# A hybrid encoder step: the attention output stays on the chip, branch B's input is split by column halves, and DeltaNet's key transposes ask for free banks

## The chip, the cores and the metric

One NeuronCore of a Trainium2 chip runs the whole program: TensorE (PE) for matrix products, VectorE (DVE), ScalarE (ACT) and GpSimd (POOL) for elementwise work, SyncE (SP) to issue most transfers. The metric is the device time of one execution in microseconds (us), the median over runs.

## The reference

One layer over 528 prompt rows (16 learned rows and 512) and 64 rows of a second sequence, width 1024, in float32. Two token mixers run in parallel on one projection and are merged under gates; a squared-ReLU MLP follows.

```python
h = rmsnorm(x, norm1)
qa, ka, va, qkv_b, z_b, beta_b, alpha_b, gate_a, gate_b = split(h @ w_in)
# A: differential attention, 8 heads, two 64-wide softmax maps per head, 128-wide values
o_a = rmsnorm((softmax(q1 k1 + bias) - lam * softmax(q2 k2 + bias)) @ va, sub_norm) * (1 - lam_init)
# B: gated DeltaNet, 8 heads of 128, causal conv of width 4, delta rule in blocks
o_b = rmsnorm(gated_delta(silu(conv(qkv_b)), g, beta, state), gdn_norm) * silu(z_b)
mix = sigmoid(gate_a + b0) * (o_a @ w_br_a) + sigmoid(gate_b + b1) * (o_b @ w_br_b)
x = x + mix @ w_out
x = x + square(relu(rmsnorm(x, norm2) @ w_up)) @ w_down
```

Outputs are the new rows of both sequences, the normed keys and the values, the DeltaNet states and the last rows before the convolution.

## The kernel before

Every float32 product of a projection is made of three fast ones: each operand is split into a high part (ScalarE copies it into `float32r`) and a low part (VectorE or GpSimd subtracts), and `feat` (line 470 on) accumulates high x high, high x low and low x high over eight 128-row blocks. A projection task covers 256 output features: two feature blocks by two halves of the 576 columns, four PSUM groups of 24 products each. Three banks of PSUM (`pg`) serve these, five (`pt`, handed out in a ring by `bank`) serve everything else. `split` makes both parts of an activation.

The order of the instructions on each engine is fixed when the program is built. `stream` emits the projection tasks in a list: DeltaNet's q, k, v, its output gate z, the attention projections, the gates GB and GA, then `br_b_tasks` (w_br_b), `br_a_tasks` (w_br_a), w_out and the MLP. After each group of eight products (`QUANTUM`) `drive` lets every waiting side chain emit its next step if a planner, `Pace`, holds it to be ready. `Pace` carries an estimated time for each engine and for the last use of each buffer; `Tags.when(tag, n)` says by that estimate when the next n buffers of a ring are free. For an operation of ScalarE that reads PSUM the planner takes 50 + 0.83 ns for each column.

The side chains that matter here:

- `delta(g)`, two halves of four heads. Its first loop transposes keys and queries of five row tiles into two banks each (`pk`, `pq`); ScalarE squares the eight 128-column blocks (`djk`) and VectorE copies the keys (`ktok`).
- `attend_prep(hd)` loads q, k, v of a head from DRAM, norms and transposes them (`ptk`, `ptq`); it waits for head hd - 3 to be finished (`oa{hd - 3}`). `attend` runs 40 units, five for each head: scores, softmax, weights transposed (`pwT`), values (`ppo`). A unit waits until the planner holds the banks of its scores to be free; the transposes and the values do not ask. `finish(hd)` norms a head's output, transposes it (`pot`), scales it into `oaT` and stores that to `oa_d`.
- `load_ob` loads DeltaNet's output (`ma`). When the last product of the last gate task has been emitted (`hidden`), it splits it into `hh` and `hl`, the buffers of the layer's own input, and only then does the first task of `br_b_tasks` begin.
- `load_oa` splits the attention output, loaded again from `oa_d` by eight transfers of GpSimd's queue after the attention stage, into `oh` and `ol`, for `br_a_tasks`.

`HELD = 3` of the four w_br_b tasks run beside attention; the fourth waits for the attention pool to close (`merge`). Evacuating a task multiplies by the gate (`thb`, `tha`), which is loaded from DRAM when the evacuation starts. `VG` picks VectorE or GpSimd for a subtraction by the planner's times; in the attention stage and from `tail` on it always picks VectorE.

Of the kernel before, what the change touches and what calls it, by code (L numbers as in the profile page):

```python
# [8 lines left out]
F32 = mybir.dt.float32  # L9
# [8 lines left out]
P = 128  # L18
KC = 8
# [191 lines left out]
def stream_step_kernel(  # L211
# [75 lines left out]
    def VG(out, n):  # L287

        if "tail" in done or "attn" in done and "merge" not in done:
            return V  # L290
        return V if max(pace.t["DVE"], pace.t["PE"]) + 1.05 * n <= max(pace.t["POOL"], pace.t["PE"]) + out * n else G
# [178 lines left out]
    def feat(xh, xl, nm, evac, m=P, ms=(0, P), halves=QHALVES, after="start", last=None, turn=False):  # L470

        def body(w):
# [3 lines left out]
            for h, (a, b) in parts:  # L476
# [4 lines left out]
                for kc in range(KC):  # L481
                    for ww, xx in ((w[0], xh), (w[0], xl), (w[1], xh)):
                        xk = xx[kc] if isinstance(xx, list) else xx[:, kc]
# [105 lines left out]
    oa_d, mb_d = ([dp.tile([P, TQ], F32, name=f"{nm}{j}") for j in range(KC)] for nm in ("oa_d", "mb_d"))  # L589
# [292 lines left out]
    def delta(g):  # L882
# [20 lines left out]
        for s in range(NT + 1):  # L903
            if s < NT:
# [342 lines left out]
    def attend_prep(hd):  # L1247
# [4 lines left out]
        q, k, v = x = [ab_.tile([P, NT, P], F32, name=f"{'qkv'[i]}{hd}", tag="qk" if i < 2 else "v") for i in range(3)]  # L1252
# [50 lines left out]
    def attend():  # L1303
# [78 lines left out]
        def finish(hd):  # L1382
# [8 lines left out]
            oaT = ab_.tile([P, TQ], F32, name=f"oaT{hd}", tag="oaT")  # L1391
            for us in ((0, 1, 2, 3), (4,)):
# [6 lines left out]
                S.activation(oaT[:, b0:b0 + w], ps[:, :w], AF.Copy, scale=sub_col)  # L1399
            store(oa_d[hd], oaT)  # L1400
# [29 lines left out]
    def load_ob():  # L1430
# [4 lines left out]
        for j in range(KC):  # L1435
            obs.append(ab_.tile([P, TQ], F32, name=f"ma{j}", tag="ob"))
            Q.dma_start(obs[j], ob_d[j][:, N0:T])
            yield
        while "hidden" not in done:
            yield  # L1440
        for j in range(KC):
            split(ob[0][:, j], ob[1][:, j], obs[j])
        done.add("ob")

    def br_b_tasks():
        out = []
        for c in range(4):
            def evac(h, ps, a, b, c=c):
                j = 2 * c + h
                if a == 0:  # L1450
                    gts["b"] = gp.tile([P, TQ], F32, name=f"thb{j}", tag="gth")
                    Q.dma_start(gts["b"], th_d[1][j])
                th = gts["b"]
# [4 lines left out]
            def body(w, c=c, evac=evac):  # L1458
                yield from feat(ob[0], ob[1], f"bb{c}", evac)(w)
                if c == 3:  # L1460
                    done.add("br_b")
            out.append(Task(f"bb{c}", w_br_b[0], c * 256, body, has("ob") if c < HELD else has("merge")))
        return out

    def br_a_tasks():
        out = []
        for c in range(4):
            def evac(h, ps, a, b, c=c):
                j = 2 * c + h
                if a == 0:  # L1470
                    gts["a"] = [gp.tile([P, TQ], F32, name=f"{nm}{j}", tag="gth") for nm in ("tha", "mbr")]
                    Q.dma_start(gts["a"][0], th_d[0][j])
                    Q.dma_start(gts["a"][1], mb_d[j])
                th, mb = gts["a"]
# [6 lines left out]
            def body(w, c=c, evac=evac):  # L1481
                yield from feat(late["oh"], late["ol"], f"ba{c}", evac)(w)
                if c == 3:
                    done.add("br_a")
            out.append(Task(f"ba{c}", w_br_a[0], c * 256, body, has("oa")))
# [3 lines left out]

    def load_oa():  # L1490
        for a in late["oa"]:
            yield pace.free(a)
            j = late["oa"].index(a)
            split(late["oh"][j], late["ol"][j], a)
        done.add("oa")
# [196 lines left out]
    with pool("delta", side="right") as db_:  # L1692
# [5 lines left out]
        drive(lambda: not chains and has("delta0", "delta1")())  # L1698
    with pool("attn", side="right") as at_:
        ab_ = Tags(pace, at_, qk=4, v=3, past=3, sc=SC, mx=6, wT=WT, ob=8, aoss=3, bias=2, osb=3,  # L1700
# [4 lines left out]
    early_cm.__exit__(None, None, None)  # L1705
    with pool("mix", side="right") as mp:
        for nm in ("mxh", "mxl"):
            late[nm] = [mp.tile([P, TQ], F32R, name=f"{nm}{j}", tag=f"{nm}{j}") for j in range(KC)]
        with pool("merge", side="right") as mg_:
            mg = Tags(pace, mg_, oa=8, xt=2)  # L1710
            late["oa"] = [mg.tile([P, TQ], F32, name=f"oa{j}", tag="oa") for j in range(KC)]
            for j in range(KC):
                G.dma_start(late["oa"][j], oa_d[j])
            for nm in ("oh", "ol"):
                late[nm] = [mg.tile([P, TQ], F32R, name=f"{nm}{j}", tag=f"{nm}{j}") for j in range(KC)]
            done.add("merge")
            chains.append(Chain(load_oa()))
# [69 lines left out]
```

## Time and profile before

| | |
|---|---|
| median of 3 runs (lowest, highest) | 1310.2 us (1308.87, 1312.29) |
| the profiled execution's own time | 1310.16 us |
| its span, first to last instruction | 1308.4 us |
| TensorE busy | 1276.9 us, 98% of the span |
| VectorE, ScalarE, GpSimd busy | 861.3, 603.4, 122.1 us |
| granted TensorE clock, mean | 0.996 of full |

Times in the trace count from the first instruction. The attention stage lies at some 585 to 786 us, the merge (w_br_a) at 798.6 to 861.2, w_out at 861.2 to 912.6, the MLP behind it. A matmul's busy time is modelled, and successive ones overlap: one of 288 columns is shown as 0.30 us, and the next starts 0.133 us later. [...]

### The profile page before, as it was taken

To read this page: it belongs to the slowest core of one execution; us is meant where nothing else is said; L and a number is where in the kernel's file an instruction comes from. 1 tells how busy PE (TensorE), PEld (TensorE's weight loads), DVE (VectorE), ACT (ScalarE), POOL (GpSimd) and SP (SyncE) were. 2 spreads that over 40 slices of the span, in tenths; PEclk is the share of its full clock that TensorE was granted. 3 is DMA by queue.
4 is the path that set the end of the run, shared out by engine and by line. 5 is a ranking of instruction groups with operands and counts; after the bars stand their busy time and mean duration, and the time that the engine had idled before them with its cause. 6 is when DMAs were issued, how large, how long until landed. Compare 5 with 4: busy or idle time off the path is not lost.

```text
span 1308.4 us, 25758 instructions
## 1 busy us (share of the span) xinstructions
PE 1276.9 (98%) x10177; PEld 1235.0 (94%) x10177; DVE 861.3 (66%) x1883; ACT 603.4 (46%) x1421; POOL 122.1 (9%) x219
## 2 busy tenths in 40 slices
PE   6999999999999999999998998999999999999998
PEld 5989999999999999998887998999999999999998
DVE  5756999434477624557778764345678678678687
ACT  5565554433643343236676742333453453443442
POOL 3111423200022000000000013300000000000000
PEclk9999999999999999999999999999999999999999
DMA  6324244532654422676454446532223313323322
GB/s 164 97 68 143 69 132 128 158 94 66 208 167 131 140 85 67 185 209 215 135 157 135 155 167 212 188 103 81 80 82 97 104 58 97 113 64 98 98 77 77
DMA packets 167422, 160.48 MB, mean 123 GB/s; under 512 B 24587, under 2 KB 148765, under 8 KB 167302
## 3 DMA queue, kind: packets, MB, share of 16 engines
q1 hardware_dynamic: 164550, 150.68, 38.0%
q0 software_dynamic: 2752, 8.16, 2.1%
q8 instruction: 80, 1.31, 0.4%
q14 instruction: 40, 0.33, 0.1%
HBM read 123.94 MB, written 37.81 MB: 124 GB/s over the span
## 4 chain that ended last, share of the span: by engine, by line
PE 86%; DMA 4%; DVE 3%; ACT 3%; issue 3%; POOL 1%; SPq 0%; DVEq 0%; ACTq 0%; POOLq 0%
PE pg_u L165 16%; PE pg_a L165 12%; PE pg_d L165 9%; PE pg_g L165 7%; PE pg_ba L165 4%; PE pg_z L165 4%; PE pg_o L165 4%; PE pd_dn L165 4%; PE pc_dn L165 4%; PE pa_dn L165 4%; PE pg_bb L165 3%; PE ppo L165 2%; PE pb_dn L165 2%; DMA bias_d<-bv_d 2%; PE po L165 1%
## 5 line engine op out<-in xcount | busy, mean ns | idle before, releaser
L165 PE MATMUL pg_u<-h2h,wh_u 128*128 128x288 f32 x512 | 151.5, 296 | 0.0
L165 PE MATMUL pg_u<-h2h,wl_u 128*128 128x288 f32 x512 | 151.3, 296 | 0.0
L165 PE MATMUL pg_u<-h2l,wh_u 128*128 128x288 f32 x512 | 151.3, 296 | 0.0
L165 PE MATMUL pg_a<-wh_a,hh 128*128 128x256 f32 (+1 forms) x480 | 136.3, 284 | 1.0 <-ACT sq L165 1.0
L165 PE MATMUL pg_a<-wh_a,hl 128*128 128x256 f32 (+1 forms) x480 | 135.8, 283 | 0.0
L165 PE MATMUL pg_a<-wl_a,hh 128*128 128x256 f32 (+1 forms) x480 | 135.5, 282 | 0.0
L165 PE MATMUL pg_d<-hl,wh_d 128*128 128x336 f32 (+1 forms) x384 | 115.4, 300 | 0.3 <-DVE hl L165 0.3
L165 PE MATMUL pg_d<-hh,wh_d 128*128 128x336 f32 (+1 forms) x384 | 115.3, 300 | 0.0
L165 PE MATMUL pg_d<-hh,wl_d 128*128 128x336 f32 (+1 forms) x384 | 115.3, 300 | 0.0
L165 PEld LDWEIGHTS pg_u<-h2h,wh_u 128*128 128x128 f32 x512 | 96.1, 188 | 0.1
L165 PEld LDWEIGHTS pg_u<-h2l,wh_u 128*128 128x128 f32 x512 | 96.1, 188 | 0.0
L165 PEld LDWEIGHTS pg_u<-h2h,wl_u 128*128 128x128 f32 x512 | 96.1, 188 | 0.0
L165 PEld LDWEIGHTS pg_a<-wh_a,hh 128*128 128x128 f32 (+1 forms) x480 | 86.5, 180 | 1.7 <-ACT sq L165 1.2
L165 PEld LDWEIGHTS pg_a<-wh_a,hl 128*128 128x128 f32 (+1 forms) x480 | 86.6, 181 | 0.5 <-issue 0.3
L165 PEld LDWEIGHTS pg_a<-wl_a,hh 128*128 128x128 f32 (+1 forms) x480 | 86.5, 180 | 0.3 <-issue 0.2
L165 PE MATMUL pg_g<-hh,wl_g 128*128 128x288 f32 x256 | 77.2, 301 | 0.0
L165 PE MATMUL pg_g<-hh,wh_g 128*128 128x288 f32 x256 | 77.0, 301 | 0.0
L165 PE MATMUL pg_g<-hl,wh_g 128*128 128x288 f32 x256 | 76.8, 300 | 0.0
L165 PEld LDWEIGHTS pg_d<-hl,wh_d 128*128 128x128 f32 x384 | 72.4, 189 | 1.2 <-issue 0.6
L165 PEld LDWEIGHTS pg_d<-hh,wl_d 128*128 128x128 f32 x384 | 72.6, 189 | 0.7 <-issue 0.6
L165 PEld LDWEIGHTS pg_d<-hh,wh_d 128*128 128x128 f32 x384 | 72.4, 189 | 0.3
L165 DVE SCALAR_TENSOR_TENSOR cv_d<-pre_d,vec,cv_d 128x595 f32<-128x595 f32 x72 | 61.6, 861 | 14.7 <-ACT cv_d L165 8.0
(398 smaller groups left out, 3764.4 us busy)
## 6 DMA issues: line engine op xcount, KB each, us to landing
wr_u<-in_w_up_dram SPq DMA_DIRECT2D x32, 512.0 KB, 3.6
wr_dn<-in_w_down_dram SPq DMA_DIRECT2D x32, 512.0 KB, 3.8
wr_d<-in_w_in_dram SPq DMA_DIRECT2D x24, 512.0 KB, 4.7
wr_a<-in_w_in_dram SPq DMA_DIRECT2D x24, 512.0 KB, 3.8
wr_g<-in_w_in_dram SPq DMA_DIRECT2D x16, 512.0 KB, 4.5
at_d<-st SPq DMA_DIRECT2D x48, 128.0 KB, 2.3
th_d<-gt SPq DMA_DIRECT2D x16, 288.0 KB, 2.1
wr_z<-in_w_in_dram SPq DMA_DIRECT2D x8, 512.0 KB
```

Source lines behind the costliest of these rows:

```text
L165: r = f(*a, **kw)
```

## The change

- The parts `oh` and `ol` of a head's attention output are written straight from PSUM in `finish`, into buffers of a new pool `own` that outlives the attention pool. The store to `oa_d`, the loads and `load_oa` go. Heads 0 to 2 have buffers of their own (`oa`); heads 3 to 6 take those of branch B's input (`ob`), and so their `finish` waits before its transposes until that input has been split; head 7 takes two of the q and k buffers.
- `load_ob` splits by column halves: eight pieces of 288 columns for the first half, then eight for the second.
- `gate_back` starts a gate's load one feature block ahead.
- The fourth w_br_b task waits for the split and the last attention unit, the w_br_a tasks for all heads, in place of pools and the reload.
- `delta` emits the next tile's transposes only once `pt.when` holds two banks to be free.
- `VG` always picks VectorE from the attention stage on.
- The pools `early` and `own` close after `tail`.

```diff
@@ -286,7 +286,7 @@
 
     def VG(out, n):
 
-        if "tail" in done or "attn" in done and "merge" not in done:
+        if "attn" in done:
             return V
         return V if max(pace.t["DVE"], pace.t["PE"]) + 1.05 * n <= max(pace.t["POOL"], pace.t["PE"]) + out * n else G
 
@@ -480,7 +480,7 @@
                 n = 0
                 for kc in range(KC):
                     for ww, xx in ((w[0], xh), (w[0], xl), (w[1], xh)):
-                        xk = xx[kc] if isinstance(xx, list) else xx[:, kc]
+                        xk = xx[kc] if isinstance(xx, (list, dict)) else xx[:, kc]
                         TE.matmul(ps[:m, :b - a], ww[:, kc, ms[h]:ms[h] + m], xk[:, a:b], start=n == 0, stop=n == 3 * KC - 1)
                         n += 1
                         if n % QUANTUM == 0 and n < 3 * KC:
@@ -586,7 +586,7 @@
     th_d = [[dp.tile([P, TQ], F32, name=f"th_d{i}{j}") for j in range(KC)] for i in range(2)]
     qkv_d = [[dp.tile([P, 640 if i == 2 else T], F32, name=f"qkv_d{i}{j}") for j in range(4)] for i in range(3)]
     at_d = [dp.tile([H, P, NT, P], F32, name=f"at_d{i}") for i in range(3)]
-    oa_d, mb_d = ([dp.tile([P, TQ], F32, name=f"{nm}{j}") for j in range(KC)] for nm in ("oa_d", "mb_d"))
+    mb_d = [dp.tile([P, TQ], F32, name=f"mb_d{j}") for j in range(KC)]
     z_d = [dp.tile([4, P, TQ], F32, name=f"z_d{g}") for g in range(2)]
     ob_d = dp.tile([H, P, T], F32, name="ob_d")
     m_d = [dp.tile([4, 20, 32, 32], F32, name=f"m_d{i}") for i in range(2)]
@@ -901,6 +901,8 @@
         G.memset(ss, 1.0)
         pks = {}
         for s in range(NT + 1):
+            while s < NT and pt.when("pt", 2) > pace.t["PE"] + BANK:
+                yield
             if s < NT:
                 c0, n = TILES[s]
                 pks[s] = [bank(f"p{x}{g}{s}").rearrange("p (h d) -> p h d", h=4) for x in "kq"]
@@ -1249,7 +1251,8 @@
         p, h = divmod(hd, 2)
         while not has(f"q{p}", f"k{p}", f"v{p}", *[f"set{hd - 2}"] * (hd > 1), *[f"oa{hd - 3}"] * (hd > 2))():
             yield
-        q, k, v = x = [ab_.tile([P, NT, P], F32, name=f"{'qkv'[i]}{hd}", tag="qk" if i < 2 else "v") for i in range(3)]
+        q, k, v = x = [(ow if i < 2 else ab_).tile([P, NT, P], F32, name=f"{'qkv'[i]}{hd}", tag="qk" if i < 2 else "v")
+                       for i in range(3)]
         for i in (1, 0, 2):
             G.memset(x[i][64:P, 0], 0.0)
             Q.dma_start(x[i][0:80, 0], at_d[i][hd, 0:80, 0])
@@ -1388,7 +1391,13 @@
             for u, (q0, n, _) in enumerate(UNITS):
                 V.tensor_scalar(osb[:n, u], osb[:n, u], r[:n, u:u + 1], None, ALU.mult)
             yield
-            oaT = ab_.tile([P, TQ], F32, name=f"oaT{hd}", tag="oaT")
+
+            while hd > 2 and "ob" not in done:
+                yield
+            tag = "oa" if hd < 3 else "ob" if hd < H - 1 else "qk"
+            parts = [ow.tile([P, TQ], F32R, name=f"o{x}{hd}", tag=tag) for x in "hl"]
+            for x, o in zip(("oh", "ol"), parts):
+                late.setdefault(x, {})[hd] = o
             for us in ((0, 1, 2, 3), (4,)):
                 ps = bank(f"pot{hd}{us[0]}")
                 b0 = QTILES[us[0]][0]
@@ -1396,8 +1405,9 @@
                     q0, n = QTILES[u]
                     TE.transpose(ps[:, q0 - b0:q0 - b0 + n], osb[:n, u], ident[:n, :n])
                 w = q0 + n - b0
-                S.activation(oaT[:, b0:b0 + w], ps[:, :w], AF.Copy, scale=sub_col)
-            store(oa_d[hd], oaT)
+                oh, ol = (o[:, b0:b0 + w] for o in parts)
+                S.activation(oh, ps[:, :w], AF.Copy, scale=sub_col)
+                V.scalar_tensor_tensor(ol, ps[:, :w], sub_col, oh.bitcast(F32), ALU.mult, ALU.subtract)
             done.add(f"oa{hd}")
 
         def unit(i):
@@ -1433,33 +1443,45 @@
             yield
         obs = []
         for j in range(KC):
-            obs.append(ab_.tile([P, TQ], F32, name=f"ma{j}", tag="ob"))
+            obs.append(ow.tile([P, TQ], F32, name=f"ma{j}", tag="ob"))
             Q.dma_start(obs[j], ob_d[j][:, N0:T])
             yield
         while "hidden" not in done:
             yield
-        for j in range(KC):
-            split(ob[0][:, j], ob[1][:, j], obs[j])
+
+        for a, b in QHALVES:
+            for j in range(KC):
+                split(ob[0][:, j, a:b], ob[1][:, j, a:b], obs[j][:, a:b])
         done.add("ob")
+
+    def gate_back(x, j):
+
+        if (x, j) not in gts:
+            pl, tag = (gp, "gth") if x == "b" else (mg, "ga")
+            gts[x, j] = [pl.tile([P, TQ], F32, name=f"{nm}{j}", tag=tag) for nm in (("thb",) if x == "b" else ("tha", "mbr"))]
+            for t, src in zip(gts[x, j], (th_d["ab".index(x)][j], mb_d[j])):
+                Q.dma_start(t, src)
+        return gts[x, j]
 
     def br_b_tasks():
         out = []
         for c in range(4):
             def evac(h, ps, a, b, c=c):
                 j = 2 * c + h
-                if a == 0:
-                    gts["b"] = gp.tile([P, TQ], F32, name=f"thb{j}", tag="gth")
-                    Q.dma_start(gts["b"], th_d[1][j])
-                th = gts["b"]
+                if a == 0 and j + 1 < KC:
+                    gate_back("b", j + 1)
+                th, = gate_back("b", j)
                 V.scalar_tensor_tensor(th[:, a:b], th[:, a:b], 1.0, ps, ALU.add, ALU.mult)
                 if b == TQ:
                     store(mb_d[j], th)
 
             def body(w, c=c, evac=evac):
+                if c == 0:
+                    gate_back("b", 0)
                 yield from feat(ob[0], ob[1], f"bb{c}", evac)(w)
                 if c == 3:
                     done.add("br_b")
-            out.append(Task(f"bb{c}", w_br_b[0], c * 256, body, has("ob") if c < HELD else has("merge")))
+            out.append(Task(f"bb{c}", w_br_b[0], c * 256, body, has("ob") if c < HELD else has("ob", f"unit{NU * H - 1}")))
         return out
 
     def br_a_tasks():
@@ -1467,11 +1489,9 @@
         for c in range(4):
             def evac(h, ps, a, b, c=c):
                 j = 2 * c + h
-                if a == 0:
-                    gts["a"] = [gp.tile([P, TQ], F32, name=f"{nm}{j}", tag="gth") for nm in ("tha", "mbr")]
-                    Q.dma_start(gts["a"][0], th_d[0][j])
-                    Q.dma_start(gts["a"][1], mb_d[j])
-                th, mb = gts["a"]
+                if a == 0 and j + 1 < KC:
+                    gate_back("a", j + 1)
+                th, mb = gate_back("a", j)
                 V.scalar_tensor_tensor(th[:, a:b], th[:, a:b], 1.0, ps, ALU.add, ALU.mult)
                 if b == TQ:
                     V.tensor_tensor(th, th, mb, ALU.add)
@@ -1479,20 +1499,15 @@
                     done.add(f"ba{j}")
 
             def body(w, c=c, evac=evac):
+                if c == 0 and "merge" in done:
+                    gate_back("a", 0)
                 yield from feat(late["oh"], late["ol"], f"ba{c}", evac)(w)
                 if c == 3:
                     done.add("br_a")
-            out.append(Task(f"ba{c}", w_br_a[0], c * 256, body, has("oa")))
+            out.append(Task(f"ba{c}", w_br_a[0], c * 256, body, has(*[f"oa{h}" for h in range(H)])))
         return out
 
     late = {}
-
-    def load_oa():
-        for a in late["oa"]:
-            yield pace.free(a)
-            j = late["oa"].index(a)
-            split(late["oh"][j], late["ol"][j], a)
-        done.add("oa")
 
     def residual():
 
@@ -1696,25 +1711,20 @@
         chains += [Chain(delta(g)) for g in range(2)]
         chains.append(Chain(conv_out()))
         drive(lambda: not chains and has("delta0", "delta1")())
+    own_cm = pool("own", side="right")
+    ow = Tags(pace, own_cm.__enter__(), oa=6, ob=8, qk=4)
     with pool("attn", side="right") as at_:
-        ab_ = Tags(pace, at_, qk=4, v=3, past=3, sc=SC, mx=6, wT=WT, ob=8, aoss=3, bias=2, osb=3,
+        ab_ = Tags(pace, at_, v=3, past=3, sc=SC, mx=6, wT=WT, aoss=3, bias=2, osb=3,
                    aqT0=2, aqT1=2, akT0=2, akT1=2)
         done.add("attn")
         chains += [Chain(attend_prep(hd)) for hd in range(H)] + attend() + [Chain(load_ob())]
         drive(lambda: "ob" in done and not chains)
-    early_cm.__exit__(None, None, None)
     with pool("mix", side="right") as mp:
         for nm in ("mxh", "mxl"):
             late[nm] = [mp.tile([P, TQ], F32R, name=f"{nm}{j}", tag=f"{nm}{j}") for j in range(KC)]
         with pool("merge", side="right") as mg_:
-            mg = Tags(pace, mg_, oa=8, xt=2)
-            late["oa"] = [mg.tile([P, TQ], F32, name=f"oa{j}", tag="oa") for j in range(KC)]
-            for j in range(KC):
-                G.dma_start(late["oa"][j], oa_d[j])
-            for nm in ("oh", "ol"):
-                late[nm] = [mg.tile([P, TQ], F32R, name=f"{nm}{j}", tag=f"{nm}{j}") for j in range(KC)]
+            mg = Tags(pace, mg_, ga=4, xt=2)
             done.add("merge")
-            chains.append(Chain(load_oa()))
             drive(has("br_b"))
             hp_cm.__exit__(None, None, None)
             xp = ctx.enter_context(pool("x1"))
@@ -1729,6 +1739,8 @@
         late["h2h"], late["h2l"] = ([h2.tile([P, TQ], F32R, name=f"h2{x}{j}", tag=f"h2{x}{j}") for j in range(KC)] for x in "hl")
         done.add("tail")
         drive(lambda: "norm2" in done and not chains)
+    own_cm.__exit__(None, None, None)
+    early_cm.__exit__(None, None, None)
     with pool("mlp", side="right") as ml:
         done.add("mlp")
         drive(has("up", "u15"))
```

## Rows read from the trace of the kernel before

**Rows 1.** The page: span, and busy time of TensorE.

```profile
span 1308.4 us, 25758 instructions
...
PE 1276.9 (98%) x10177; PEld 1235.0 (94%) x10177; DVE 861.3 (66%) x1883; ACT 603.4 (46%) x1421; POOL 122.1 (9%) x219
```

**Rows 2.** Waits of TensorE, whole span: us in total, times, longest.

```profile
PE pg_ba L165 <- DVE ol L165: 4.5, 2, 2.3
PE pk L165 <- DVE ktok L165: 2.1, 2, 1.4
PE ptk L165 <- DVE mx L165: 2.0, 1, 2.0
...
PE pg_bb L165 <- ACT hh L165: 1.7, 1, 1.7
...
PE pg_bb L165 <- DVE hl L165: 0.4, 1, 0.4
```

**Rows 3.** Windows, merge and w_out: us, then busy (instructions) of each engine, clock.

```profile
798.60:861.20 62.60, 58.11 (x428) 56.95 (x427) 25.09 (x36) 17.75 (x25) 19.07 (x11) 0.97 0.60 191
861.20:912.60 51.40, 51.40 (x386) 51.26 (x386) 27.27 (x39) 17.70 (x23) 0.00 (x0) 1.00 0.27 83
...
806.00:808.00 2.00, 2.00 (x8) 1.76 (x8) 1.31 (x3) 0.00 (x0) 0.00 (x0) 0.50 0.88 217
808.00:810.00 2.00, 2.00 (x14) 2.00 (x14) 0.00 (x0) 0.00 (x0) 0.00 (x0) 0.79 0.90 255
```

**Rows 4.** Timeline of VectorE, start of the merge: start, us, operation.

```profile
801.36 4.92 DVE L165 TENSOR_TENSOR ol<-oa,oh 128x576 fp32r<-128x576 f32 x3
```

**Rows 5.** Timeline of ScalarE and VectorE at the start of w_br_b.

```profile
706.21 4.68 ACT L165 CAST hh<-ma 128x576 fp32r<-128x576 f32 x8
710.79 0.49 ACT L165 ACTIVATE gt<-pg_g,bgh 128x288 f32<-128x288 f32 x1
711.18 0.73 ACT L165 COPY wT<-pwT 128x256 f32<-128x256 f32 x2
...
706.89 5.44 DVE L165 TENSOR_TENSOR hl<-ma,hh 128x576 fp32r<-128x576 f32 x8 [0.23 <-ACT hh L165]
...
726.24 0.45 DVE L165 SCALAR_TENSOR_TENSOR thb<-thb,pg_bb 128x288 f32<-128x288 f32 x1
726.61 1.22 DVE L165 TENSOR_TENSOR wl_bb<-wr_bb,wh_bb 128x1024 fp32r<-128x1024 f32 x1
727.74 0.95 DVE L165 SCALAR_TENSOR_TENSOR aqT<-ptq,vec,aqT 128x464 fp32r<-128x464 f32 x2
```

**Rows 6.** DeltaNet's key transposes: a wait of TensorE, and readers of `pk` (ns min/median/max).

```profile
95.74 1.11 PE L165 MATMUL pk<-ident,kT 128*128 128x128 f32 x4 [1.35 <-DVE ktok L165]
...
L165 ACT ACTIVATE djk<-pk x40: 257/277/289, 84.8 to 360.3; 128x128 f32<-128x128 f32 x32, 80x128 f32<-80x128 f32 x8
L165 ACT ACTIVATION_READ_ACCUMULATOR djk<-pk x40: 190/194/223, 84.9 to 360.4; 128x1 f32 x32, 80x1 f32 x8
```

**Rows 7.** Windows in DeltaNet, in attention and behind its wait; columns as above.

```profile
97.00:99.00 2.00, 2.00 (x10) 2.00 (x9) 0.76 (x2) 1.84 (x11) 0.00 (x0) 0.54 0.05 12
675.00:700.00 25.00, 25.00 (x204) 22.75 (x203) 19.87 (x71) 17.75 (x55) 1.44 (x10) 1.00 0.48 151
720.00:722.00 2.00, 2.00 (x10) 1.55 (x11) 0.03 (x1) 1.99 (x5) 0.02 (x1) 0.52 0.99 363
```

**Rows 8.** Timelines of SyncE and TensorE, the last heads of attention.

```profile
701.16 0.86 SPq L165 DMA_DIRECT2D k<-at_d  x2
...
729.69 0.85 SPq L165 DMA_DIRECT2D k<-at_d  x2
...
773.51 0.65 PE L165 MATMUL ppo<-past,wT 128*64 128x128 f32 x4
...
782.82 0.80 PE L165 MATMUL pot<-ident,osb 128*128 128x128 f32 x5
```

## The prediction

> **What bounds the kernel now.** I read the page first, then TensorE's waits over the whole span, then windows around each wait. TensorE is busy 1276.9 of the 1308.4 us [rows 1], and the change leaves every matmul of it in place: no product of a projection, of a score or of a DeltaNet block is added or taken away. So the time can move only by what TensorE stands idle (31.5 us, about half of it before the first projection and after the last, where nothing is touched) and by the stretches in which its granted clock is at half. The waits that the change can reach are few [rows 2]: 4.5 us where the merge's first task waits for the low part of the attention output, 2.1 us where DeltaNet's key transposes wait for a bank, 2.0 us where an attention head's key transposes do, and 2.1 us where branch B's first task waits for its own input. In the merge the reader is to see more than the wait: behind it the clock is granted at 0.50, then 0.79, with 8 and 14 matmuls in 2 us [rows 3], where the next stage, of equal products, does 386 in 51.4 us at full clock, 0.133 us each, thus 15 in 2 us.
>
> **The change part by part.**
> *Attention output kept on the chip.* Removed: eight stores, eight loads, and in the merge 8 splits on ScalarE and 8 on VectorE. These came late: the loads follow the last heads' stores, and VectorE evacuates branch B in between. Three of the last low parts take it from 801.36 to 806.3 us [rows 4], and TensorE consumes them as they come. With both parts written as each head ends, the merge's first task finds all of them there: the last head's values end at 774.2 us [rows 8], the first merge product starts at 798.6 [rows 3], and the 24 us between cover the last head's norm, transposes and two evacuations. Gained: the wait of 4.5, and the half clock behind it, (15 - 8) x 0.133 + (15 - 14) x 0.133 = 1.1 and some 0.5 for the clock's fall before it: 6.1. From above: this stage takes 62.6 us against 51.4 for the next, and its 42 instructions more, the residual's transposes, explain at 0.16 us each (five take 0.80 [rows 8]) 6.7 of the 11.2, at 0.1 each, the least I would set, 4.2; so 4.5 to 7.0 is left. The wait alone is 4.5, if the clock falls anyway. I take 6.1, since the clock is full before and after.
>
> The low part now comes from PSUM, on VectorE in the attention stage: a pair of the same shapes to some 10% takes 0.95 us [rows 5], so 8 x 0.95 = 7.6 us more on VectorE, in a stage where it is busy 19.9 of 25 us [rows 7]. TensorE has the held-back gate and branch-B products to run beside it, and of all the waits above one only of 2.0 us is for VectorE within attention [rows 2]. If none of the 7.6 shows, 0; if all, 7.6. I take 0.6, nearer the first, because attention ends 11 us before it is needed (below).
>
> *Branch B's input by halves.* The splits of eight 576-column pieces take 4.68 us on ScalarE and 5.44 on VectorE, 0.585 and 0.68 each; TensorE uses a piece in 3 x 0.133 = 0.40 us, so it is paced by VectorE. A 288-column instruction runs at a pitch of 711.18 - 710.79 = 0.39 on ScalarE and 726.61 - 726.24 = 0.37 on VectorE [rows 5]. Sixteen take 6.2 and 5.9 us, thus 1.5 and 0.5 more on the engines, but the first eight, all that the first product group needs, keep up with TensorE. Gained: 0.2 on the first cast, 0.3 on the first low part, 6 x 0.17 = 1.0 between pieces (the 0.28 of VectorE's excess, less what attention's own instructions fill). Head 3's five transposes, 0.8 us [rows 8], now are issued into the wait itself, because its finish waits for this point and precedes the first product. Sum 2.3; bounds 0 (the longer total gives it back) and 2.3 + 2.0 + 1.4 = 5.7, if the wait of 2.0 us for a bank [rows 2] and the half clock behind it (0.52 granted, 10 instructions in 2 us [rows 7]) go too. They may: head 6's transposes come later now. I leave them in, because the work before them on VectorE stays (5.9 and 0.95 in place of 5.4, with head 6's two norms moved behind).
> A ScalarE piece at 0.39 us stays under the 0.40 that TensorE needs [rows 5]. [...]
>
> *Who else waits.* Heads 3 to 6 write into the buffers of branch B's input, so finish(3) waits for its split. Queued behind it: head 6's loads, because they need `oa3`. Today they issue at 701.16 [rows 8]; now some 6 us later, behind the seam, with the memsets on GpSimd and twelve transfers on SP following. Its norms run on VectorE directly behind the split, which ends at 712.3 today [rows 5], so they lose only 2 to 3 us. That is covered by the 11 us below.
>
> *DeltaNet's transposes.* TensorE waits 1.35 us at 95.7 [rows 6] and loses the clock behind it (0.54 for 2 us [rows 7]); 0.7 us in the other half. The new loop asks the planner whether both banks are free and lets projections go first. The planner prices a square of 128 PSUM columns on ScalarE at 50 + 0.83 x 128 = 156 ns; measured are 277 ns and 194 ns for its accumulator [rows 6], so eight take 2.2 to 3.8 us, not 1.25. It will often think the banks free. One held group of eight products (1.2 us) nearly covers the first wait. Bounds: 0 and 2.1 + 1.4 = 3.5; I take 1.4, the named wait, and leave the clock.
>
> *At nothing.* Gate loads one feature block ahead remove VectorE's waits, which are already counted. Eight wl_ba lowers and up to three wl_o move from GpSimd to VectorE, 1.2 us each [rows 5], where the splits (8 x 0.69) leave; VectorE is busy 25 of 62.6 us there [rows 3], and three product banks cover an evacuation 1.2 us late. Without that cover each would cost up to 1.2, 13 in all; I take none. Closing pools later moves no work.
>
> **Sum.** 1310.16 (span 1308.4 and 1.8 around it, the median of the runs) - 6.1 - 2.3 - 1.4 + 0.6 = 1301.0 us. Within 0.3%, 1306.3 to 1314.1, is what a measurement here can't tell from no change.
>
> **The rivals.**
> 1. *All seams close:* the 2.0 us wait, both DeltaNet waits and the clock behind them also go: 1301.0 - 3.4 - 2.1 = 1295.5. For it: the same engines cause them. Against: the planner's price of the squares.
> 2. *Only the merge gains:* the planner finds the banks free, the split's longer total takes back its start: 1310.2 - 6.1 + 0.6 = 1304.7.
> 3. *A block at branch B's seam:* head 3's transposes hold two of five banks until ScalarE has done sixteen pieces (706.2 + 6.2 = 712.4) and VectorE its own and the pair (714). The next ungated attention transposes that get one of these banks stop all TensorE: from 708 at the earliest, 6 us, and 1.6 for the clock: 1308.6, no change. For it: a bank held behind VectorE stopped TensorE 2.0 us here [rows 2]. Against: three other banks serve the next weights' transposes and values. [...]
> 4. *Slower: attention's tail becomes the bound.* The last quarter of branch B now waits for the last unit, and the merge for all heads. Today the third quarter ends at 798.6 - 51.4 / 4 = 785.7, against 774.2 for the last values: 11.5 us to spare. A slip of S costs S - 11.5 + 1.6. It decides against the change from S = 13.1 + 11.5 - 1.6 = 23 us on (to 1314.1). Head 6's and head 7's loads lie 28.5 us apart [rows 8]; losing most of such a turn does it, and a whole one gives 1301.0 + 18.6 = 1319.6. For it: head 6 now hangs on the seam. Against: its delay counts to 2 or 3 us.
>
> **Chances.** The forecast 0.47 (its own range 1298 to 1306), rival 1 0.13, rival 2 0.13, rival 3 0.15, rival 4 0.12. Faster are the forecast and rivals 1 and 2: 0.73; rival 3 is the same: 0.15; slower 0.12. The range, 1295 to 1309, leaves out rival 4 and the low end of rival 1, some 0.16, and holds the unknown bounds of the split (0 to 5.7), of DeltaNet (0 to 3.5) and most of VectorE's added work (0 to 7.6).
>
> **What would show it.** Right: the wait of the merge's first products for `ol` is gone and the clock is full through the stage, which shrinks from 62.6 to about 56.5 us; the first branch-B products run without gaps; the wait before the key transposes at 95.7 is under half. Wrong: a TensorE wait of several us on a transpose of attention between branch B's first and second task (rival 3); a gap before the last quarter of branch B or before the merge (rival 4); more waits for VectorE within attention (the 0.6 too small); unchanged DeltaNet waits (rival 2). What would overturn all of it is an order that shifts elsewhere, since every estimate of the planner behind a moved instruction moves with it.

## The result and the profile after

The changed kernel takes 1301.0 us (median of four executions, 1299.7 to 1303.4) against 1311.2 us (1308.9 to 1312.5) for the kernel before on the same chip: ratio 0.9933, 95% interval 0.9920 to 0.9945. The forecast was 1301.0 us. The profiled execution is the slowest of the four (1303.4 us), so its stages show 7 of the 10 us.

The page of the changed kernel answers to [rows 1]: TensorE is busy as long as before, on as many instructions, and the span is 7.1 us shorter. VectorE has 8 us more, though not by the low parts: those from PSUM take 8.2 us and replace splits of 10.7. What adds time is the low parts of w_br_a's weights, 9.7 us, which came over from GpSimd.

```profile
span 1301.3 us, 25712 instructions
...
PE 1275.9 (98%) x10177; PEld 1234.9 (95%) x10177; DVE 869.3 (67%) x1910; ACT 597.9 (46%) x1419; POOL 96.0 (7%) x202
```

TensorE's waits over the whole span, beside [rows 2]: the wait for `ol` is gone, the one for DeltaNet's keys is unchanged, the attention bank's has fallen from 2.0 to 0.4, and the one for branch B's input has grown.

```profile
PE pg_bb L165 <- ACT hh L165: 2.5, 1, 2.5
PE pk L165 <- DVE ktok L165: 2.1, 2, 1.4
...
PE ptk L165 <- DVE mx L165: 0.4, 1, 0.4
```

Windows of the changed kernel, columns as in [rows 3]: the merge from its first product to w_out's first, 2 us of its start, and then 8 us at the start of branch B.

```profile
798.70:854.20 55.50, 55.50 (x425) 55.04 (x425) 26.61 (x38) 17.44 (x25) 1.58 (x3) 1.00 0.59 176
...
802.00:804.00 2.00, 2.00 (x17) 2.00 (x17) 1.59 (x2) 0.00 (x0) 0.00 (x0) 1.00 0.48 177
712.00:714.00 2.00, 1.45 (x5) 1.25 (x6) 1.47 (x4) 2.00 (x8) 0.00 (x0) 0.54 0.00 0
714.00:716.00 2.00, 2.00 (x11) 2.00 (x11) 2.00 (x7) 2.00 (x7) 0.00 (x0) 0.50 0.03 8
716.00:718.00 2.00, 2.00 (x10) 1.55 (x9) 2.00 (x6) 2.00 (x7) 0.00 (x0) 0.50 0.00 0
718.00:720.00 2.00, 2.00 (x12) 2.00 (x13) 1.86 (x8) 1.97 (x6) 0.00 (x0) 0.75 0.38 147
```

The merge is as forecast: no gap, clock 1.00 throughout. Branch B's start is not. Timelines of ScalarE, VectorE and TensorE there, beside [rows 5]:

```profile
711.53 0.55 ACT L165 ACTIVATE sc<-sc,mx 64x320 f32<-64x320 f32 x1
711.99 0.19 ACT L165 ACTIVATION_READ_ACCUMULATOR sc<-sc,mx 64x1 f32 x1
712.08 5.42 ACT L165 CAST hh<-ma 128x288 fp32r<-128x288 f32 x16
...
712.53 5.99 DVE L165 TENSOR_TENSOR hl<-ma,hh 128x288 fp32r<-128x288 f32 x16 [1.47 <-ACT hh L165]
...
712.55 0.61 PE L165 MATMUL pg_bb<-hh,wh_bb 128*128 128x288 f32 x1 [2.53 <-ACT hh L165]
```

ScalarE comes to the casts at 712.08, 5.9 us later than before, for two reasons. The last gate product starts 3.1 us later (708.04 against 704.95), behind more of attention's work. And from that product to the first cast pass 4.0 us in place of 1.3, because ScalarE is busy with exps of attention from 708.73 on; before, too, exps stood there, but fewer. TensorE has 2 us of attention work after the gate product, stands 2.53 us, and runs at a granted clock of 0.50 to 0.54 for the next 6 us.

To compare the runs below, each profile is divided at three products of TensorE: the first of w_g, of w_br_a and of w_out. "Attention" is the first stretch, in which branch B runs too; "merge" is the second. (The window of [rows 3] ends 0.2 us later than this merge.)

```
kernel               w_g     w_br_a  w_out   attention merge | median us, ratio to before [95%]
before               592.4   798.6   861.0   206.2     62.4  |
after                592.5   798.7   854.2   206.2     55.5  | 1301.0  0.9933 [0.9920, 0.9945]
e1_nogate            591.4   796.1   851.7   204.7     55.6  | 1300.7  0.9933 [0.9920, 0.9945]
e2_keep              590.7   800.4   856.0   209.7     55.6  | 1310.1  0.9996 [0.9984, 1.0008]
e3_notkept           594.7   797.0   852.8   202.3     55.8  | 1302.4  0.9937 [0.9921, 0.9954]
e4_whole             590.7   797.1   852.6   206.4     55.5  | 1302.3  0.9952 [0.9936, 0.9967]
e5_nopre             591.1   797.8   853.4   206.7     55.6  | 1302.1  0.9924 [0.9896, 0.9952]
e6_pre               592.3   797.0   852.9   204.7     55.9  | 1303.2  0.9930 [0.9902, 0.9958]
e7_halves            593.5   795.7   859.1   202.2     63.4  | 1308.4  0.9969 [0.9949, 0.9988]
e8_gate25            596.4   801.4   857.0   205.0     55.6  | 1305.9  0.9960 [0.9940, 0.9981]
e9_first             592.8   798.1   853.6   205.3     55.5  | 1302.8  0.9948 [0.9934, 0.9961]
e10_notkept_first    591.3   801.0   856.9   209.7     55.9  | 1306.8  0.9976 [0.9966, 0.9986]
e11_gpsimd           590.6   792.0   847.5   201.4     55.5  | 1296.8  0.9899 [0.9886, 0.9912]
e12_notkept_gpsimd   593.7   798.9   854.8   205.2     55.9  | 1303.3  0.9945 [0.9930, 0.9960]
```

The column w_g shows how far one execution differs from another before anything of attention has run: up to 2.3 us either way, apart from e8. The changed kernel and e1, which turn out to be the same program, differ by 1.5 us in the attention stage; a smaller difference in one profile says nothing.

### The profile page after: what moved, and what is told of

Read it like the earlier page. It is cut to its first block, busy times and chain, and to the rows that moved or that the text cites. A ratio compares the mean times of both kernels' runs of the same rounds, so it can differ in the third digit from the quotient of the medians.

```text
span 1301.3 us, 25712 instructions
## 1 busy us (share of the span) xinstructions
PE 1275.9 (98%) x10177; PEld 1234.9 (95%) x10177; DVE 869.3 (67%) x1910; ACT 597.9 (46%) x1419; POOL 96.0 (7%) x202
## 4 chain that ended last, share of the span: by engine, by line
PE 87%; DVE 4%; DMA 3%; ACT 3%; issue 2%; SPq 1%; POOL 0%; DVEq 0%; ACTq 0%; POOLq 0%
PE pg_u L165 16%; PE pg_a L165 11%; PE pg_d L165 9%; PE pg_g L165 7%; PE pg_ba L165 4%; PE pg_bb L165 4%; PE pg_z L165 4%; PE pg_o L165 4%; PE pd_dn L165 4%; PE pa_dn L165 4%; PE pc_dn L165 4%; PE ppo L165 2%; PE pb_dn L165 2%; DMA bias_d<-bv_d 2%; PE po L165 1%
```

## The experiments

**The DeltaNet loop left out** (e1):

```diff
-            while s < NT and pt.when("pt", 2) > pace.t["PE"] + BANK:
-                yield
```

> The changed kernel without the DeltaNet loop that asks for free banks. Theory: the planner prices a square at 156 ns and never holds a transpose back, so both programs issue the same instructions in the same order, and the time is that of the changed kernel, 1301 us, ratio to the kernel before 0.992 to 0.995, with the same two waits of TensorE for the copy of the keys (1.4 and 0.7 us). Rival, as the prediction had it: the loop saves one wait, and without it 1.4 us are lost, about 1302.5 us, with longer waits than 1.4 us.

Measured: ratio 0.9933, the changed kernel's own. The theory held. The wait for DeltaNet's keys is 2.1 us with and without the loop, and the program with the loop issues the same instructions in the same order on every engine as the one without. The planner always takes the banks to be free: this part of the change does nothing.

**Only the kept output** (e2: whole pieces, gates loaded as before, no loop, the old choice of engine in the merge), **everything but the kept output** (e3: halves, branch B's gates ahead, new choice of engine, no loop), and **whole pieces in the changed kernel** (e4):

```diff
 e2, on the changed kernel: e1's and e4's lines, and
-                if a == 0 and j + 1 < KC:
-                    gate_back("b", j + 1)
...
-        if "attn" in done:
+        if "tail" in done or "attn" in done and "merge" not in done:
 e3, on the kernel before: e6's lines below, e4's the other way round, and
-        if "tail" in done or "attn" in done and "merge" not in done:
+        if "attn" in done:
 e4, on the changed kernel:
-        for a, b in QHALVES:
-            for j in range(KC):
-                split(ob[0][:, j, a:b], ob[1][:, j, a:b], obs[j][:, a:b])
+        for j in range(KC):
+            split(ob[0][:, j], ob[1][:, j], obs[j])
```

> The kernel before with one part of the change alone, the attention output kept on the chip: no halves, no gate loads ahead, no bank question, GpSimd chosen as before. Theory: this part carries the gain, since the wait of the merge for its low parts and the half clock behind it are all that went away: 6 to 7 us less than before, 1304 to 1305 us, and a merge of 55 to 56.5 us. Rival: the merge also needs the gates loaded ahead and the lowers on VectorE, without which its start stays late: at most 3 us less than before, 1308 us or more, with a wait left at the first merge products.

> The kernel before with everything but the kept output: halves, branch B's gates loaded ahead, VectorE always; the attention output still goes through DRAM (the merge's own gates are loaded as before, and the DeltaNet loop is left out). Theory: the wait of 4.5 us in the merge stays, and the halves bring what the prediction gave them at most, so 1309 to 1312 us, ratio 0.998 to 1.002. Rival: the blocked VectorE in the merge was the cause, and gates loaded ahead free it, so that the low parts come in time: 1304 to 1306 us with the output still through DRAM.

> The changed kernel with branch B's input split in whole 576-column pieces, as before. Theory as in the prediction: the halves save 2.3 us at the start of the first branch-B product group, so this takes 1303.3 us, with gaps of some 0.17 us between the first products. Rival from the trace of the changed kernel: ScalarE's softmax work before the split sets the start (a wait of 2.5 us, longer than before), so the halves bring at most 1 us, 1301 to 1302 us.

My theory, that the kept output carries the gain, fell. Alone it closes the merge (55.6 us) and yet the kernel is no faster (0.9996): its attention stage is 3.5 us longer in the profile, which is the fastest of twelve executions, and most executions lose more. Of the twelve, those with a mean granted clock of 0.997 or more take 1305.0 to 1306.8 us, those at 0.992 to 0.995 take 1308.7 to 1312.3. That the clock is what they lose goes by these means alone, since one execution was profiled. Where the attention stage loses is seen in TensorE's waits of e2:

```profile
PE pg_bb L165 <- ACT hh L165: 2.8, 1, 2.8
PE pwT L165 <- DVE sc L165: 2.7, 1, 2.7
```

and in its timeline: the second wait lies at attention's end, where the last quarter of branch B is held back until the last unit has run. (Counted from the first product of w_g, e2 has issued as many matrix instructions as the kernel before after 180 us, 1373 and 1371, and 23 fewer after 195 us.)

```profile
782.15 0.74 PE L165 MATMUL pwT<-ident,sc 128*128 128x128 f32 x5 [2.74 <-DVE sc L165]
...
785.75 0.65 PE L165 MATMUL ppo<-past,wT 128*64 128x128 f32 x4 [0.45 <-DVE wT L165]
```

That is the mechanism of the prediction's rival 4, in small. The run without the kept output (e3) has the merge's gain all the same: 55.8 us, with the attention output still stored, loaded and split late. So the loads and stores were not what made `ol` late. And beside all the rest, keeping the output changes the time by 1.4 us (e3 against the changed kernel) with overlapping intervals: no gain of it is shown. e4 is 1.6 us above e1, which differs by the halves alone; it lies between its two expectations, and the intervals overlap.

**The changed kernel without gate loads ahead** (e5), **the kernel before with branch B's gate loads ahead and nothing else** (e6), **with the halves and nothing else** (e7):

```diff
 e5, on the changed kernel (the same for "a"):
-                if a == 0 and j + 1 < KC:
-                    gate_back("b", j + 1)
...
-                if c == 0:
-                    gate_back("b", 0)
 e6, on the kernel before:
-                if a == 0:
-                    gts["b"] = gp.tile([P, TQ], F32, name=f"thb{j}", tag="gth")
-                    Q.dma_start(gts["b"], th_d[1][j])
-                th = gts["b"]
+                if a == 0 and j + 1 < KC:
+                    back(j + 1)
+                th = back(j)
```

(`back(j)` makes that tile and starts that load once; `back(0)` is called ahead of the first product. e7 is e4's edit the other way round, on the kernel before.)

> The changed kernel with the gates loaded as in the kernel before (each at its own evacuation), all else as changed. Theory A: loading branch B's gate one feature block ahead keeps attention off VectorE's wait for that load, so without it the tail of attention slips and the last quarter of branch B waits for the last unit: a wait of TensorE for the scores or values at 775 to 787 us, 1305 to 1310 us. Rival B: the kept output and the halves carry the gain: 1300 to 1302.5 us and no such wait.

> The kernel before with one edit: branch B's gate is loaded one feature block ahead. Theory A: VectorE no longer stands behind that load, the low parts of the attention output are ready before the merge needs them, its first products don't wait, the merge takes 55 to 56.5 us in place of 62.6: 1301.5 to 1304 us in all. Rival B: the load isn't what delays the low parts (their own loads or the order on VectorE is): the merge stays at 60 us or more, 1307 to 1310 us.

> The kernel before with one edit: branch B's input is split by halves (sixteen pieces of 288 columns). Theory A (the recorded term): 2.3 us less, 1306.5 to 1308, with the merge still 62 us and its wait for the low part still there. Rival B: the halves give nothing by themselves, since ScalarE is late with something else: 1308.5 to 1310.

e6 shows what had held `ol` back. VectorE's waits from 780 to 810 us, first the kernel before, then e6:

```profile
DVE thb L165 <- DMA thb<-th_d: 13.1, 3, 6.2
```

```profile
DVE thb L165 <- PE pg_bb L165: 7.7, 5, 3.6
```

Before, VectorE stands 13.1 us behind three loads of branch B's gate, each issued only at its own evacuation, and splits into `ol` are queued behind these evacuations. With the loads one block ahead, the evacuations of branch B wait only for TensorE's products (w_br_a's own gate loads still hold VectorE for 6.1 us there, but behind the last split), TensorE's wait for `ol` is gone, and the merge falls from 62.4 to 55.9 us with that one edit (ratio 0.9930). With the output kept there is no split left to be late (e5: 55.6 us without gate loads ahead). Each of the two edits closes the merge's gap by itself; together they close it once. In e5 theory A fell: attention's tail is not bound there, though the gates are loaded late. e4, whose pieces are whole and whose gates are loaded ahead, has no such wait either: only e2, which lacks both the halves and the early loads, has the wait of 2.7 us at attention's end. How either of them prevents it was not traced.

The halves alone (e7) shorten the attention stage by 4.0 us, and the merge still waits 4.5 us for `ol`; the ratio, 0.9969, has an interval of 1.6 to 6.7 us, and the time, 1308.4, lies between the two expectations. Between 700 and 720 us TensorE's instructions number 55 + 60 before, and in e7 and e3:

```profile
700.00:710.00 10.00, 8.47 (x59) 6.76 (x59) 6.37 (x26) 8.17 (x29) 0.15 (x1) 0.95 0.57 177
710.00:720.00 10.00, 10.00 (x75) 9.69 (x74) 9.62 (x30) 7.61 (x21) 0.82 (x6) 0.88 0.29 86
```

```profile
700.00:710.00 10.00, 8.47 (x64) 6.65 (x63) 5.45 (x24) 7.01 (x25) 0.15 (x1) 0.99 0.58 179
710.00:720.00 10.00, 10.00 (x72) 9.81 (x73) 9.62 (x31) 8.61 (x24) 0.82 (x6) 0.84 0.32 108
```

In the changed kernel the second ten microseconds hold 35, at a clock of 0.66:

```profile
700.00:710.00 10.00, 10.00 (x82) 8.09 (x80) 6.47 (x27) 6.17 (x21) 1.59 (x10) 1.00 0.53 171
710.00:720.00 10.00, 7.47 (x35) 6.80 (x34) 8.39 (x27) 9.94 (x32) 0.00 (x0) 0.66 0.08 31
```

What the kept output takes from the halves is 3.9 us from e3 to the changed kernel (2.4 to e1), and most of it is lost at this one seam: counted from the first product of w_g, the changed kernel is 8 matrix instructions ahead of e3 after 115 us, 24 behind after 130, and 28 behind after 195.

**A loop in DeltaNet that does hold** (e8):

```diff
-            while s < NT and pt.when("pt", 2) > pace.t["PE"] + BANK:
+            while s < NT and pt.when("pt", 2) + 2500 > pace.t["PE"] + BANK:
```

> The changed kernel with 2.5 us added to the time at which DeltaNet's loop takes the banks to be free, so that it lets projections go first. Theory A (the mechanism of the change is good, only its estimate of the squares is too low): the waits of 1.4 and 0.7 us for the banks and the half clock behind them go, 1.4 to 3.5 us less than the changed kernel: 1297.5 to 1299.5. Rival B: DeltaNet's chain then ends later, or the wait moves to another transpose: within 1 us of the changed kernel, or above it.

The named waits and the clock behind them do go: from 90 to 120 us TensorE issues 209 instead of 192 instructions, at 1.00 instead of 0.94. But the chain is late afterwards, and the next stretch has 156 instead of 217. Windows of the changed kernel, of e8, then a wait of e8:

```profile
90.00:120.00 30.00, 28.43 (x192) 26.38 (x191) 20.00 (x45) 20.97 (x87) 6.55 (x17) 0.94 0.34 104
120.00:150.00 30.00, 28.72 (x217) 27.55 (x216) 22.86 (x37) 15.93 (x34) 12.15 (x14) 1.00 0.40 136
```

```profile
90.00:120.00 30.00, 29.08 (x209) 27.56 (x209) 20.15 (x43) 20.81 (x84) 5.55 (x16) 1.00 0.38 120
120.00:150.00 30.00, 22.89 (x156) 22.18 (x155) 18.14 (x32) 12.62 (x26) 12.51 (x12) 0.83 0.30 98
```

```profile
PE pkn L165 <- DVE ktok L165: 7.1, 1, 7.1
```

Rival B held: the wait moved to the next transposes, and grew. (In the profiles whose loop does not hold, this wait is at most 3.1 us.)

**The split asked first** (e9 on the changed kernel, e10 on e3), and **the first half's high casts on GpSimd** (e11 on the changed kernel, e12 on e3):

```diff
 e9: the split becomes a chain of its own, ahead of attention's
-        chains += [Chain(attend_prep(hd)) for hd in range(H)] + ...
+        chains += [Chain(split_ob())] + [Chain(attend_prep(hd)) for hd in range(H)] + ...
 e11, inside the loop over halves and j:
+                if a:
+                    split(ob[0][:, j, a:b], ob[1][:, j, a:b], obs[j][:, a:b])
+                else:
+                    G.tensor_scalar(ob[0][:, j, a:b], obs[j][:, a:b], 1.0, 0.0, ALU.mult, ALU.add)
+                    V.tensor_tensor(ob[1][:, j, a:b], obs[j][:, a:b], ob[0][:, j, a:b].bitcast(F32), ALU.subtract)
```

> The changed kernel with the split of branch B's input in a chain of its own that is asked first, so that its casts are issued ahead of the exps of the attention unit that now precede them on ScalarE; the same instructions otherwise. Theory A: what the kept output costs at this seam (a wait of 2.5 us where the kernel before had 1.4 to 2.1, and half clock behind it) is the order on ScalarE, so the wait falls to 1.5 us or less, and 1.5 to 4 us go: 1297 to 1299.5. Rival B: the casts then wait for the last gate products, whose buffers they write, or for the low parts on VectorE, and the clock falls anyway: 1300 to 1302.

> The kernel of the run e3 (halves, branch B's gates ahead, output through memory) with the same chain asked first. Theory A: its seam, which waits 1.4 us, has 3 us of exps ahead of the casts as well: the wait falls under 0.7 us and the clock holds, 1298 to 1301. Rival B: nothing moves, since the gate products end at 707.5 in any case: 1301.5 to 1303.

> The changed kernel with the eight high casts of the first half on GpSimd, which is idle there, in place of ScalarE. Theory A: ScalarE, busy with exps until 712.1, is all that the first product waits for: the first product of branch B starts 1.5 to 3 us earlier, 1297.5 to 1299.5. Rival B: GpSimd's cast takes longer than the 0.40 us that TensorE needs per piece, so TensorE waits for each piece at half clock: 1301 to 1305.

> The kernel of the run e3 (halves, branch B's gates ahead, attention output through memory) with the eight high casts of the first half on GpSimd, as in e11. Theory A: what the kept output costs lies at branch B's seam alone, so with the seam closed by GpSimd's casts the two ways of handing over the attention output are worth the same: 1296 to 1298. Rival B: the kept output costs elsewhere too (its low parts on VectorE, head 6's later loads), so without it the kernel is faster than e11 by 2 us or more: under 1295. Rival C: GpSimd gains less here, because the wait that it can remove is 1.4 us and not 2.5: 1299 to 1302.

e9 starts the casts 1.5 us earlier, but one unit's values, transposes and scores, the 2 us of work that TensorE had ahead of the wait, now stand behind it: the wait is 2.4 us, and the clock falls again, to 0.58 and 0.57 in the 4 us from 712 to 716. Two exps still precede the casts. Order alone gains nothing (1302.8 us, above both expectations). In e10 the wait of 1.4 us stays, though the clock is 1.00 from 700 to 716 us, as its theory had it; but the same edit opens waits of 4.5 us in two on the weights' transposes, which VectorE's maxima release, and the time, 1306.8 us, is above both expectations:

```profile
718.98 1.52 PE L165 MATMUL pwT<-ident,sc 128*128 128x128 f32 x7 [2.49 <-DVE mx L165]
```

e11 is the fastest kernel of this study: 1296.8 us, 0.9899 [0.9886, 0.9912], some 4 us below the changed kernel and a little more than its theory promised. Timelines of its GpSimd, ScalarE and TensorE:

```profile
700.52 3.39 POOL L165 TENSOR_SCALAR hh<-ma 128x288 fp32r<-128x288 f32 x8
...
710.15 2.75 ACT L165 CAST hh<-ma 128x288 fp32r<-128x288 f32 x8
...
709.55 0.40 PE L165 MATMUL pg_bb<-hl,wh_bb 128*128 128x288 f32 x1 [1.14 <-DVE hl L165]
```

GpSimd takes 0.42 us a piece where ScalarE takes 0.34, but it has nothing queued: its casts are done at 703.9, while TensorE is at the gate products of the other column half, which end at 706.4 and don't read what the casts write. What is left is 1.1 us for the first low part, and the clock stays at 1.00.

e12 has the same edit without the kept output. Its seam keeps a wait of 1.70 us at a clock of 1.00 (from 700 to 780 us), but at attention's end the last head's norm stands on VectorE behind an evacuation that waits for TensorE, and TensorE waits for that head's transposes. Its timeline and the window behind:

```profile
783.63 1.22 PE L165 MATMUL pot<-ident,osb 128*128 128x128 f32 x5 [2.86 <-DVE osb L165]
```

```profile
784.00:787.00 3.00, 3.00 (x13) 2.60 (x13) 0.26 (x2) 2.41 (x4) 0.00 (x0) 0.54 0.76 297
```

All three expectations missed: it is slower than e11, by 6.0 us (ratios) to 6.5 us (medians), for a reason that none of them had, and no faster than e3. Whether the kept output would be worth anything if neither tail nor seam waited is thus open.

## Why the prediction came out right

Its total and its direction held, and so did the size of the merge's term; the others missed by amounts that cancel. That it met the median to a tenth of a microsecond is luck: it forecast 9.2 us less than 1310.2, and 10.3 less than 1311.2 were measured.

- **The merge, -6.1.** Measured -6.9, by the mechanism named: the wait of 4.5 us and the clock of 0.50 and 0.79 behind it [rows 3] are gone. But the cause given was wrong in part. It named the loads of the output, which follow the last heads' stores, and VectorE's evacuations in between. The loads were not it: VectorE stood behind the gate loads (13.1 us), and e6 gains 6.5 us of the merge with the output still in memory. Beside the kept output the early gate loads are indeed worth next to nothing, since their gain is "already counted" (e5: a merge of 55.6 us without them). The step that failed is the credit: the gain was put down to the kept output, which alone leaves the time at 0.9996, and not to the gate loads, which alone reach 0.9930, as much as the whole change within the intervals.
- **The halves, -2.3.** By themselves 4.0 in the attention stage, within the bounds of 0 to 5.7. In the changed kernel the start that the term was built on is not there: the casts begin 5.9 us later than before, 3.1 of it because the last gate product is later and the rest behind exps. Head 3's transposes come at 716.6, after the first eight products and not into the wait. Against whole pieces the halves are worth 0.2 to 1.7 us here (e4 against the changed kernel and e1), hardly more than two profiles of one program differ by. Rival 3 had put a block at this seam, by banks held in PSUM; the seam did lose time, but to ScalarE's queue.
- **The size of a piece.** 5.42 us for sixteen is 0.34 us on ScalarE, and 5.99 is 0.37 on VectorE. A single piece on ScalarE is shown with a median of 428 ns, but successive pieces overlap, and what counts against TensorE's 0.40 us is the 0.34. TensorE is not paced by either engine in e10, at a clock of 1.00: the products of the first half follow at 0.13 us each, without a gap, once they have begun.
- **Low parts from PSUM, +0.6.** The kept output costs the attention stage 3.5 us (before to e2, at its end) to 3.9 us (e3 to after, at the seam). That the 8.2 us of low parts on VectorE do it is not shown: at the seam VectorE had finished by 711.1, and the casts waited for ScalarE. That the late casts cost the changed kernel time is shown by e11, which takes half of them off ScalarE and gains 4.2 us. Why more exps stand there with the kept output than before was not traced; e9 undid a part of that order and gained nothing.
- **DeltaNet, -1.4.** Nothing. The prediction named the reason, a planner that prices the squares too low, and still took the term; e8 shows that a loop that does hold loses 3.5 us (by the ratios) to 5 us (by the medians).
- **Head 6 "some 6 us later", norms "2 to 3".** Its loads issue at 702.84, 1.7 us later, since SyncE was not held up; its norms run at 724.73, 12.5 us later than before, because the split itself is late. The last values move from 773.5 [rows 8] to 782.9, which uses 9.4 of the 11.5 us to spare. (These 11.5 were some 0.4 too many: the last two products of values in the kernel before run from 774.09 on and end at 774.5.) In e2 they start at 785.75, with TensorE's wait of 2.74 us ahead of them. Rival 4 was closer than its 0.12 said.
- **GpSimd's lowers on VectorE, at nothing.** Not run alone. Where its gap is closed, the merge takes 55.5 to 55.9 us with them on VectorE, and 55.6 (e2) and 55.9 (e6) with the old choice, so nothing speaks against the term.

In sum, the terms in the attention stage were -1.7 and came out at 0 (after) to -1.5 (e1, the same program); the merge gave 0.8 more, DeltaNet 1.4 less. From profile to profile that is 6.9 to 8.3 us. The median of the kernel before lay 1.1 us above its profiled execution and that of the changed kernel 2.4 us below its own, which makes up the rest.

## What to carry to other kernels

When a wait ends on an engine, ask what that engine stood behind: here loads issued at the moment of use held VectorE up for 13.1 us, ahead of unrelated splits in the same queue, and issuing them one step earlier closed the gap as fully (a merge of 55.9 us) as taking the splits away (55.6). Two edits that each close the same gap are worth one of them, so test each alone before adding their terms. At a seam where the tight engine gets to its work late, an engine that is slower per piece but idle can win: GpSimd's 0.42 us against 0.34 saved 4 us in the changed kernel. In e3's kernel the same edit saved nothing, because the next wait along the way opened (e12).

## What the runs showed of the hardware

The same wait is dear or cheap by what the clock does behind it, and its length does not decide that here. Waits of 2.53 us (after), 2.44 us (e9) and 2.86 us (e12) were followed by windows of 2 to 3 us at 0.50 to 0.58. But the wait of 2.74 us in e2 was followed by 1.00, and waits of 1.4 to 1.7 us went either way: those of e3 and e6 were followed by 0.50, those of e10, e12 and the kernel before by 1.00. First e2 behind its wait, then branch B's start in the kernel before and in e6, which has the same wait of 1.7 us there, then e3:

```profile
782.00:784.00 2.00, 1.78 (x13) 1.51 (x14) 1.80 (x8) 1.97 (x8) 0.00 (x0) 1.00 0.47 156
```

```profile
708.00:710.00 2.00, 1.99 (x14) 1.52 (x14) 2.00 (x4) 2.00 (x5) 0.18 (x2) 1.00 0.06 24
```

```profile
708.00:710.00 2.00, 2.00 (x10) 1.80 (x10) 2.00 (x4) 2.00 (x4) 0.00 (x0) 0.50 0.30 119
```

```profile
710.00:712.00 2.00, 2.00 (x11) 1.98 (x10) 2.00 (x7) 2.00 (x7) 0.20 (x3) 0.50 0.58 225
```

So an edit that removes a wait can gain the wait alone or the stretch behind it (0.50 to 0.58 here) too, and one execution doesn't tell which. In e2, whose code is the same in every execution, the mean granted clock lay anywhere from 0.992 to 0.999 and the time from 1305.0 to 1312.3 us. What decides when the clock falls was not found.
